# Second score product of 64-wide heads over all 128 rows, with k's low parts copied into both halves of their tile

## The chip, the cores and the metric

The kernel runs on one core of one Trainium2 chip. The metric is the device time of one execution in microseconds; the time of the kernel before is the median of three runs. A profile of one further execution, with a trace of every instruction, was taken by the hardware profiler.

## What is computed

Two transformer blocks on one sequence of 512 tokens and 1024 features, all in float32. The first block joins a sparse attention (compressed, selected and window branches for 16 heads of 64 in four groups of keys and values) with a linear recurrent branch, then a gated feed-forward part. The second block has two layers, each with a feed-forward part, four mixers side by side, and another feed-forward part. Three of the mixers matter here, cut to their score products:

```python
# neighbourhood attention: 4 heads, d = 64, a window of 8 x 32 keys for each column block
logits = jnp.einsum('brcqhd,brkcjhd->brcqhkj', qg, kg,
                    preferred_element_type=jnp.float32) * (d ** -0.5) + bias
# grouped-query attention: 4 heads, 2 of keys and values, d = 64
logits = jnp.einsum('bqngd,bknd->bngqk', qb, k, preferred_element_type=jnp.float32) * scale
# multi-head latent attention: 4 heads, d = 64 + 32 = 96
logits = jnp.einsum('bqhd,bkhd->bhqk', q, k, preferred_element_type=jnp.float32) * scale
```

Each is followed by a softmax and a product with the values. The fourth mixer, differential attention, has heads of 32.

## The kernel before

**Split products.** Every float32 operand of a product is split in two float32r parts, high (ScalarE's copy) and low (VectorE's difference). A product is the sum high x high + high x low + low x high in one PSUM bank. For large weights these are the three matmuls of `feat` (L142 to L144) and `tok_` (L172 to L174), over 128 rows each.

**Scores of 64-wide heads.** The features of a head stand on 64 partitions, so q's two parts share one tile of 128 partitions, [high; low] (`pair_T`, `q_pair`). k's high part stands twice in its tile, [high; high]: ScalarE writes the upper half (L754 in `kdup`, L1515 in `k_both`), POOL copies it to the lower (`again`, L747, called from `kdup`; L1516). k's low part stands only in the upper half of its tile, written by VectorE (L756, L1517); nothing is written in its lower half. The first product, over 128 rows, gives high x high and low x high together. The second takes the upper 64 rows of q's tile and k's low part, high x low, and adds it into the same bank:

- first block: L1571 and L1572, once for each of 16 heads, 2 branches and 4 blocks of queries (128 pairs); the columns are 128, 256, 384 and 512, by block of queries;
- grouped-query attention: L1025 and L1026, 16 pairs of 512 columns in each layer;
- neighbourhood attention: both on L1097, in a loop over k's two tiles with r = 128 and r = 64 rows, 16 pairs of 256 columns in each layer.

Latent attention multiplies over 96 rows (L1224 to L1226), differential attention over 96 rows in one product (L948).

**Order.** In the first block 32 units (group, head, branch) run in turn. In step j of a unit stand the scores and softmax of the next unit for query block j (`soft`), a piece of fill work (`fill.pump`: projections, gates), and the values of this unit (`pv`: four transposes, a split by ScalarE and VectorE, two products). `k_both` of the next group is called in unit 5 of 8, and its tiles are used from unit 7 on. In the second block 16 heads of four mixers run in turn, in the order differential, neighbourhood, grouped-query, latent; a head is prepared in the turn two before its values, its scores run in the turn one before. `kdup` is called at step 2 of that preparation for neighbourhood attention, and at step 0 of every second head for grouped-query attention. Within this order a scheduler sets the place of every instruction on its engine's queue by priorities (`high_priority`) and a simulated timeline. Each engine works its queue in order.

**POOL** in these stretches also splits the low parts of streamed weights (L127, while `attends` is set), scales P by the softmax sums (L777, L1106, L1577) and makes bias tables (L1091, L1562). Tiles for k are taken from a ring of 4 (second block) or 6 (first block) shared by high and low parts.

Of the kernel before, what the change touches and what calls it, by code (L numbers as in the profile page):

```python
# [47 lines left out]
def pick(w, m):  # L48
    """Columns of one 128-wide part, high and low."""
    return w[0][:, m * 128:m * 128 + 128], w[1][:, m * 128:m * 128 + 128]  # L50


def whole(gen):
    """Runs a generator to its end."""
    while True:
        try:
            next(gen)
        except StopIteration as e:
            return e.value


class Fill:
    """Work in small steps that is laid between the steps of other work."""
# [21 lines left out]
class Kern:  # L85
# [8 lines left out]
    # ---------------------------------------------------------------- helpers  # L94
    def weights(self, bufs):
        """A pool for parts of weights in flight."""
        self.wb = bufs
        return self.tc.tile_pool(name="w", bufs=1)
# [4 lines left out]
    def pair(self):  # L103
        """Two banks for a block of products; where no attention runs, its banks take turns with them."""
# [3 lines left out]
    def stream(self, src, K, C):  # L108
        """Loads a block [128, K*C] of weights in parts of four k-tiles, split into two float32r parts."""
# [26 lines left out]
    def feat(self, ps, w, ks, mh, ml, start=True, stop=True):  # L136
        """ps[feature, token] += w(k).T @ m(k), three passes."""
# [8 lines left out]
    def feat2(self, w, ks, mh, ml):  # L146
        """Two banks [feature, token] for a block of 256 features."""
        return whole(self.feat2_(w, ks, mh, ml))
# [10 lines left out]
    def tok(self, w, K, C, xh, xl):  # L159
        """Four [token, feature] parts of two banks: x(tb).T @ w. The first product of a bank marks all of it unwritten,  # L160
        so that the first of its second half overwrites."""
# [20 lines left out]
    def rstd(self, ss, width, n, tag, bufs=2):  # L182
        """(ss / width + eps) ** -0.5 on [128, n]."""
# [7 lines left out]
    def rstd_v(self, ss, width, n, tag, bufs=2):  # L191
        """The same on the vector engine: a first guess from the bits, then three steps of Newton's method."""
# [11 lines left out]
    def tokred(self, acc, rhs, n):  # L204
        """Sums acc [128 features, 512 tokens] over features against rhs [128, n] -> psum [128 tok, 4, n]."""
# [6 lines left out]
    def bcast(self, r, pool=None, tag="rB", bufs=1):  # L212
        """r [128 tok, 4] -> [128, 512] with r along the free axis in each partition."""
# [13 lines left out]
    def norm_k(self, xk, k, g, xh, xl, acc):  # L227
        """One k-tile of a norm: squares into acc, x*g split into xh, xl."""
# [21 lines left out]
    # ---------------------------------------------------------------- program  # L250
# [28 lines left out]
    def skews(self, pa):  # L279
        """Rows in DRAM that a strided read turns into Toeplitz tables: the negated T5 bias of each head over the  # L280
        distance from -511 to 511, 128 times."""
# [16 lines left out]
    def skews_na(self):  # L298
        """The neighbourhood bias 16 times."""
# [64 lines left out]
    def norm(self, gname, g0):  # L364
        """The norm of x by one gain: called for each k-tile once it is final, then finished."""
# [12 lines left out]
    def outproj(self, w_o, mh, ml, norm):  # L378
        """x += w_o.T @ m, and the norm that follows."""
# [10 lines left out]
    def gate(self, br, j, t):  # L390
        """Twice the sigmoid, less one, of a block of a branch's gates into t."""
# [6 lines left out]
    def merge(self, pm, got, ah, al, lh, ll, mh, ml):  # L398
        """The gated sum of both branches; got: the gates that there are."""
# [24 lines left out]
    def lru(self, pl, po, yT):  # L424
# [4 lines left out]
        # softplus(-lambda), with log1p(e) = 2 artanh(e / (2 + e))  # L429
# [88 lines left out]
    def ffn(self, f, half, norm):  # L518
        """x += (half) * swiglu, and the norm that follows."""
# [36 lines left out]
    # ---------------------------------------------------------------- second block  # L556
# [18 lines left out]
    def final_norm(self, l):  # L575
        """x = rmsnorm(x) * final, and the norm by ffn1 that follows it in the next layer."""
# [52 lines left out]
    def mix(self, px, l, norm):  # L629
        """The four mixers: their projections and w_out rows fill the tensor engine between the steps of attention,  # L630
        in which the softmax of one head runs beside the values of the head before."""
# [21 lines left out]
        # ---- projections  # L653
        def proj(src, C, evac):
            """A token-major projection: evac(tb, psum, r) takes each block of 128 tokens."""
# [21 lines left out]
        def sums(t, n, d):  # L677
            """Sums of squares over d of t [128, 4, n, d]."""
# [11 lines left out]
        def rope_n(rope, t, tb, n, d):  # L690
            """Rotates t [128, n, d] of one block of tokens in place."""
# [10 lines left out]
        # ---- attention  # L702
        def transp(src, n=128):
            """Four transposes of src(tb) [128 tok, n] into one bank [n, 512 tok]."""
# [5 lines left out]
        def times(a, n):  # L710
            """a [128, d] n times side by side."""
# [17 lines left out]
        def pair_T(src, hh, of=same, to_=same):  # L729
            """[hi; lo] of one of two heads from a bank with both."""  # L730
# [6 lines left out]
        def kpair(src, g=None, n=128):  # L737
            """[hi] and [lo], times a gain by row."""
# [10 lines left out]
        def kdup(src, b, g=None):  # L749
            """Of 64 rows from a bank, at b: [hi; hi] and [lo]."""  # L750
# [5 lines left out]
            V.scalar_tensor_tensor(kl[0:64], src, g, kh[0:64].bitcast(FT), op0=OP.mult, op1=OP.subtract)  # L756
            return kh, kl
# [8 lines left out]
        def plain(ps, t, qb):  # L766
            """Softmax of the unbiased scores of one block of queries."""
# [26 lines left out]
        def finish(y, hh, of=same, to_=same):  # L794
            """Adds the two halves of O into the rows of one head in y()."""
# [8 lines left out]
        def ypair(n=2):  # L804
            """Lazily made pairs of heads."""
# [21 lines left out]
        def ynorm(y, beta):  # L827
            """rmsnorm over the 256 features of two pairs, split."""
# [3 lines left out]
        def wout(parts):  # L832
            """x += w_out rows of the mixers i, each from Y: two pairs (hi, lo)."""
# [13 lines left out]
        def wout_b(Y, sum_b):  # L847
            """The last mixer's rows, whose norm's factor follows; the first pair's products run ahead."""
# [822 lines left out]
def host(inputs):  # L1671
# [4 lines left out]
    A = {}  # L1676
# [146 lines left out]
```

## Time and profile before

| | us |
|---|---|
| median of three runs | 3197.78 |
| lowest and highest | 3192.75 and 3217.31 |
| span of the profiled execution | 3202.2 |

The page gives no time of the profiled execution other than its span, from the first to the last instruction. The engines' busy times over that span are TensorE 3109.5 us (97%), its weight loads 2569.8 us (80%), VectorE 1797.9 (56%), ScalarE 1396.5 (44%) and POOL 676.2 (21%).

PE is TensorE's matmuls, PEld its weight loads, DVE VectorE, ACT ScalarE, POOL GpSimd, SP SyncE. A matmul's duration runs from its start to a modelled end and holds its latency, so that a busy PE need not be PE at its peak; how close matmuls follow each other is read from their starts. `128*128 128x512` is a stationary tile of 128 rows by 128 columns and a moving one of 128 rows by 512 columns. PEclk is the granted clock of TensorE as a share of full speed. The column behind `|` or in brackets is idle time of the engine before an instruction, and what ended it; "issue" is time in which it waited for nothing that the profile shows.

### The profile page before, as it was taken

How to read it: one execution, taken by the hardware profiler on the slowest of the kernel's cores; microseconds unless marked ns; L12 is line 12 of the kernel's file. 1: busy time of each engine (PE TensorE's matmuls, PEld its weight loads, DVE VectorE, ACT ScalarE, POOL GpSimd, SP SyncE). 2: the span in 40 equal slices, each digit the busy share in tenths (PEclk: the TensorE clock that was granted, in tenths of full speed). 3: DMA queues.
4: the chain of work that ended last, by engine and by line, in shares of the span. 5: the costliest groups of instructions: out<-in, count | busy, mean ns of one | idle time of the engine just before them, and what ended most of it. 6: DMA issues, size and time to landing. Idle time of an engine off the chain costs nothing.

```text
span 3202.2 us, 41597 instructions
## 1 busy us (share of the span) xinstructions
PE 3109.5 (97%) x15289; PEld 2569.8 (80%) x15289; DVE 1797.9 (56%) x3520; ACT 1396.5 (44%) x2753; POOL 676.2 (21%) x726
## 2 busy tenths in 40 slices
PE   7999999999999999999999999999999999899998
PEld 6887777878888888889877788888888987678886
DVE  7566766454443444437886644445443698764433
ACT  4566665233332333336665433333333566543332
POOL 3355641010000000016652100010000556310000
PEclk9999988999999999999899999999999999999999
DMA  4211111342233332333221223322233322123332
GB/s 146 87 57 53 47 46 40 99 140 98 94 98 96 96 99 97 95 111 93 75 55 34 86 99 95 96 92 99 99 96 95 109 81 59 34 73 99 99 96 82
DMA packets 105268, 275.84 MB, mean 86 GB/s; under 512 B 27172, under 2 KB 36900, under 8 KB 104904
## 3 DMA queue, kind: packets, MB, share of 16 engines
q1 hardware_dynamic: 105064, 273.18, 27.0%
q8 instruction: 120, 1.97, 0.3%
q14 instruction: 84, 0.69, 0.1%
HBM read 268.93 MB, written 6.80 MB: 86 GB/s over the span
## 4 chain that ended last, share of the span: by engine, by line
PE 76%; issue 12%; DVE 8%; ACT 2%; POOL 1%; DMA 1%; DVEq 0%; SPq 0%; ACTq 0%; POOLq 0%
PE ps_mm L142 8%; PE ps_mm L144 8%; PE ps_mm L143 8%; PE ps_s L143 6%; PE ps_s L144 6%; PE ps_s L142 6%; PE ps_t L144 6%; PE ps_t L143 6%; PE ps_t L142 6%; PE ps_mm L172 2%; PE ps_mm L174 2%; PE ps_mm L173 2%; PE ps_s L1572 1%; PE ps_t L1590 1%; PE ps_t L787 1%
## 5 line engine op out<-in xcount | busy, mean ns | idle before, releaser
L125 ACT ACTIVATE hi<-raw 128x512 fp32r<-128x512 f32 (+2 forms) x952 | 594.8, 627 | 1356.2 <-PE ps_s L143 407.5
L127 DVE TENSOR_TENSOR lo<-raw,hi 128x512 fp32r<-128x512 f32 x782 | 547.7, 702 | 929.4 <-ACT hi L125 918.6
L142 PE MATMUL ps_mm<-xh,hi 128*128 128x512 f32 (+1 forms) x792 | 311.4, 394 | 2.3 <-ACT hi L125 2.3
L144 PE MATMUL ps_mm<-xh,lo 128*128 128x512 f32 (+1 forms) x792 | 310.1, 393 | 1.5 <-POOL lo L127 1.5
L143 PE MATMUL ps_mm<-xl,hi 128*128 128x512 f32 (+1 forms) x792 | 310.1, 391 | 0.0
L238 POOL TENSOR_TENSOR acc<-acc,sq 128x512 f32<-128x512 f32 x49 | 74.4, 1518 | 1051.3 <-issue 525.6
L142 PE MATMUL ps_s<-xh,hi 128*128 128x512 f32 x656 | 253.2, 391 | 7.5 <-ACT hi L125 7.5
L143 PE MATMUL ps_s<-xl,hi 128*128 128x512 f32 x656 | 257.3, 392 | 3.1 <-DVE xl L243 3.0
L172 PE MATMUL ps_mm<-hi,xh 128*128 128x256 f32 (+1 forms) x896 | 259.2, 292 | 0.9 <-ACT tk L664 0.7
L127 POOL TENSOR_TENSOR lo<-raw,hi 128x512 fp32r<-128x512 f32 (+2 forms) x170 | 226.1, 1334 | 150.9 <-ACT hi L125 142.5
L173 PE MATMUL ps_mm<-lo,xh 128*128 128x256 f32 (+1 forms) x896 | 256.5, 289 | 0.0
L144 PE MATMUL ps_s<-xh,lo 128*128 128x512 f32 x656 | 256.3, 391 | 0.0
L174 PE MATMUL ps_mm<-hi,xl 128*128 128x256 f32 (+1 forms) x896 | 256.1, 290 | 0.1
L142 PE MATMUL ps_t<-xh,hi 128*128 128x512 f32 x608 | 236.8, 390 | 0.0
L143 PE MATMUL ps_t<-xl,hi 128*128 128x512 f32 x608 | 236.6, 389 | 0.0
L144 PE MATMUL ps_t<-xh,lo 128*128 128x512 f32 x608 | 235.9, 390 | 0.7 <-DVE lo L127 0.5
L172 PEld LDWEIGHTS ps_mm<-hi,xh 128*128 128x128 f32 x896 | 173.7, 195 | 5.5 <-ACT tk L664 1.3
L144 PEld LDWEIGHTS ps_mm<-xh,lo 128*128 128x128 f32 (+1 forms) x792 | 148.5, 187 | 34.8 <-POOL lo L127 2.4
L142 PEld LDWEIGHTS ps_mm<-xh,hi 128*128 128x128 f32 (+1 forms) x792 | 148.6, 188 | 34.4 <-ACT hi L125 2.6
L173 PEld LDWEIGHTS ps_mm<-lo,xh 128*128 128x128 f32 x896 | 173.8, 195 | 2.9 <-issue 1.2
L174 PEld LDWEIGHTS ps_mm<-hi,xl 128*128 128x128 f32 x896 | 172.4, 194 | 4.2 <-issue 1.6
L143 PEld LDWEIGHTS ps_mm<-xl,hi 128*128 128x128 f32 (+1 forms) x792 | 148.6, 188 | 31.9 <-issue 1.4
(539 smaller groups left out, 6739.9 us busy)
## 6 DMA issues: line engine op xcount, KB each, us to landing
raw<-in_w_g SPq DMA_DIRECT2D x110, 512.0 KB
raw<-in_w_u SPq DMA_DIRECT2D x110, 512.0 KB
raw<-in_w_d SPq DMA_DIRECT2D x108, 512.0 KB
raw<-in_w_o SPq DMA_DIRECT2D x24, 512.0 KB
raw<-in_w_c SPq DMA_DIRECT2D x16, 512.0 KB
raw<-in_w_m SPq DMA_DIRECT2D x16, 512.0 KB
raw<-in_w_a SPq DMA_DIRECT2D x12, 512.0 KB
raw<-in_w_d SPq DMA_DIRECT2D x20, 256.0 KB
```

Of the source, the lines that this page charges most:

```text
L125: nc.scalar.activation(hi[:, :c], x, AF.Copy)
L127: eng.tensor_tensor(lo[:, :c], x, hi[:, :c].bitcast(FT), op=OP.subtract)
L142: mm(ps, wh, mh(km), start=s, stop=False)
L143: mm(ps, wh, ml(km), start=False, stop=False)
L144: mm(ps, wl, mh(km), start=False, stop=e)
L172: mm(out[tb], h, wh, start=k == 0 and tb % 2 == 0, stop=False)
L173: mm(out[tb], h, wl, start=False, stop=False)
L174: mm(out[tb], o, wh, start=False, stop=k == K - 1 and tb % 2 == 1)
L238: nc.gpsimd.tensor_tensor(acc, acc, sq, op=OP.add)
L787: PE.transpose(ps[:, qb * 128:qb * 128 + 128], P[qb][:, kb * 128:kb * 128 + 128], ident)
L1572: PE.matmul(ps[:, :L], q[0:64], kl[0:64, :L], start=False, stop=True)
L1590: PE.transpose(tps[:, (qb - kb) * 128:(qb - kb + 1) * 128], P[qb][:, kb * 128:kb * 128 + 128], ident)
```

## The change

The tile of k's low part is filled in both halves: after VectorE has written the upper 64 rows, POOL copies them to the lower 64 rows. The second product then runs over 128 rows of q's tile [high; low] and k's tile [low; low] and gives high x low plus low x low. The first products are as they were. The rest of the diff takes out comments and docstrings, with the line numbers kept up to the edit.

```diff
@@ -747,13 +747,14 @@
         def kdup(src, b, g=None):
...
             V.scalar_tensor_tensor(kl[0:64], src, g, kh[0:64].bitcast(FT), op0=OP.mult, op1=OP.subtract)
+            again(kl[64:128], kl[0:64])
             return kh, kl
@@ -1023,14 +1024,14 @@
                     PE.matmul(ps, qT, kh, start=True, stop=False)
-                    PE.matmul(ps, qT[0:64], kl[0:64], start=False, stop=True)
+                    PE.matmul(ps, qT, kl, start=False, stop=True)
@@ -1093,8 +1094,7 @@
                     for n, kk in enumerate(t["k"]):
-                        r = 128 - 64 * n
-                        PE.matmul(ps[:, :256], qT[0:r], kk[0:r].rearrange("p (r c) -> p r c", c=64)[:, :, c0:c0 + 32],
+                        PE.matmul(ps[:, :256], qT, kk.rearrange("p (r c) -> p r c", c=64)[:, :, c0:c0 + 32],
                                   start=n == 0, stop=n == 1)
@@ -1515,10 +1515,11 @@
                 V.scalar_tensor_tensor(kl[0:64], src, gb, kh[0:64].bitcast(FT), op0=OP.mult, op1=OP.subtract)
+                G.tensor_scalar(kl[64:128], kl[0:64].bitcast(FT), 1.0, 1.0, op0=OP.mult, op1=OP.mult)
                 t["kT"].append((kh, kl))
@@ -1569,7 +1570,7 @@
             PE.matmul(ps[:, :L], q, kh[:, :L], start=True, stop=False)
-            PE.matmul(ps[:, :L], q[0:64], kl[0:64, :L], start=False, stop=True)
+            PE.matmul(ps[:, :L], q, kl[:, :L], start=False, stop=True)
```

## Rows read from the trace of the kernel before

**Rows 1.** The page: the chain that ended last, shares of the span by engine

```profile
PE 76%; issue 12%; DVE 8%; ACT 2%; POOL 1%; DMA 1%; DVEq 0%; SPq 0%; ACTq 0%; POOLq 0%
```

**Rows 2.** Stretches: length, busy time and count by engine, granted clock, DMA share, GB/s

```profile
core 0: us, PE busy (x) PEld busy (x) DVE busy (x) ACT busy (x) POOL busy (x), PEclk, DMA share, GB/s
130.00:530.00 400.00, 392.82 (x2037) 303.67 (x2036) 263.42 (x748) 261.53 (x614) 200.23 (x211) 0.96 0.14 47
1550.00:1680.00 130.00, 121.67 (x722) 100.00 (x721) 112.96 (x306) 83.32 (x202) 85.53 (x118) 0.93 0.22 60
```

**Rows 3.** Chain that ended last, by line: 130 to 530 us, then 1550 to 1680

```profile
by line: PE ps_s L1572 11.0%; PE ps_mm L142 9.8%; PE ps_mm L144 9.5%; PE ps_mm L143 9.3%; PE ps_t L1590 9.1%; PE ps_s L1571 6.3%; PE ps_mm L172 5.5%; PE ps_mm L174 5.4%; PE ps_mm L173 5.3%; PE ps_o L1594 3.5%; PE ps_n L1594 3.2%; PE ps_o L1
...
by line: PE ps_mm L172 6.7%; PE ps_mm L174 6.1%; PE ps_mm L173 6.0%; issue 5.2%; PE ps_s L1097 4.4%; DVE st L773 4.3%; DVE PTl L225 4.2%; DVE tk L697 3.1%; PE ps_s L1026 3.0%; PE ps_t L1116 2.9%; PE ps_t L787 2.4%; DVE xT L845 2.3%; PE ps_o
```

**Rows 4.** Timeline (start us, duration us, engine, instruction): a dense stretch, 512 columns

```profile
1400.03 0.39 PE L142 MATMUL ps_t<-fh,hi 128*128 128x512 f32 x1
1400.03 0.19 PEld L143 LDWEIGHTS ps_t<-fl,hi 128*128 128x128 f32 x1
...
1400.93 0.39 PE L143 MATMUL ps_t<-fl,hi 128*128 128x512 f32 x1
```

**Rows 5.** Timeline: two products of latent attention, over 96 rows

```profile
1727.57 0.40 PE L1225 MATMUL ps_s<-kT,qT 96*128 96x512 f32 x1
1727.80 0.40 PE L1226 MATMUL ps_s<-kT,qT 96*128 96x512 f32 x1
```

**Rows 6.** Timeline: full-height steps of 256 columns (first row) and 128

```profile
231.87 0.28 PE L1593 MATMUL ps_o<-PTh,Vt 128*128 128x256 f32 x1
...
1621.55 0.27 PE L1125 MATMUL ps_o<-PTl,Vg 128*128 128x128 f32 x1
1621.66 0.28 PE L1124 MATMUL ps_o<-PTh,Vg 128*128 128x128 f32 x1
```

**Rows 7.** Timeline: pairs of 512, 256 and 128 columns, then one of L1097

```profile
220.97 0.47 PE L1571 MATMUL ps_s<-kT,qT 128*128 128x512 f32 x1
221.38 0.18 PEld L1572 LDWEIGHTS ps_s<-kT,qT 64*128 64x128 f32 x1 [0.24 <-issue]
221.38 0.50 PE L1572 MATMUL ps_s<-kT,qT 64*128 64x512 f32 x1
221.81 0.19 PEld L173 LDWEIGHTS ps_mm<-lo,xh 128*128 128x128 f32 x1 [0.25 <-issue]
221.81 0.39 PE L173 MATMUL ps_mm<-lo,xh 128*128 128x256 f32 x1
...
231.99 0.28 PE L1571 MATMUL ps_s<-kT,qT 128*128 128x256 f32 x1
232.20 0.38 PE L1572 MATMUL ps_s<-kT,qT 64*128 64x256 f32 x1
232.51 0.38 PE L172 MATMUL ps_mm<-hi,xh 128*128 128x256 f32 x1
...
140.48 0.31 PE L1571 MATMUL ps_s<-kT,qT 128*128 128x128 f32 x1
140.72 0.32 PE L1572 MATMUL ps_s<-kT,qT 64*128 64x128 f32 x1
140.97 0.33 PE L1590 MATMUL ps_t<-ident,P 128*128 128x128 f32 x1
...
1564.00 0.68 PE L1097 MATMUL ps_s<-kT,qT 128*128 128x256 f32 x2
1564.61 0.39 PE L172 MATMUL ps_mm<-hi,xh 128*128 128x256 f32 x1
```

**Rows 8.** By line: POOL's copies of k, VectorE's low part; ns min/median/max, first, last

```profile
L1516 POOL TENSOR_SCALAR kT<-kT x8: 612/616/1534, 114.4 to 426.4; 64x512 fp32r<-64x512 f32 x8
...
L747 POOL TENSOR_SCALAR kT<-kT x28: 610/614/1077, 1474.6 to 2686.1; 32x512 fp32r<-32x512 f32 x16, 64x512 fp32r<-64x512 f32 x12
...
L756 DVE SCALAR_TENSOR_TENSOR kT<-ps_t,gn,kT x8: 733/734/736, 1554.1 to 2657.3; 64x512 fp32r<-64x512 f32 x8
```

**Rows 9.** The page: POOL's splits of weights, count, busy us, mean ns

```profile
L127 POOL TENSOR_TENSOR lo<-raw,hi 128x512 fp32r<-128x512 f32 (+2 forms) x170 | 226.1, 1334 | 150.9 <-ACT hi L125 142.5
```

## The prediction

> **What bounds the kernel now.** I read the chain that ended last first: TensorE's matmuls hold 76% of it, VectorE 8%, the rest is small [rows 1]. So work taken off TensorE should shorten the run, but only where the chain stands on TensorE in the stretch concerned. The changed products run in two kinds of stretch: the attention of the first block, 130 to 530 us, and, once in each layer of the second block, neighbourhood and grouped-query attention (1550 to 1680 us in layer 0; layer 1 repeats it). The view by stretches shows the reader who else is busy there: in the first, VectorE 263 and ScalarE 262 of 400 us; in the second, VectorE 113 of 130 us, which is 87% [rows 2]. The chain of these stretches alone, by line, says how much of it is the products to be changed: L1572 11.0% in the first; L1097 4.4% and L1026 3.0% in the second, where VectorE's lines come up between them [rows 3].
>
> **What the second product costs beyond its columns.** In the timeline of the dense stretches a full-height matmul of 512 columns starts every 0.225 us (1400.03 to 1400.93, four steps), and the weights of the next one are loaded while it runs: both rows begin at 1400.03 [rows 4]. Products over 96 rows keep that pace, 0.23 us from L1225 to L1226, although both add into one bank and use the same stationary tile [rows 5]. 256 columns take 0.12 us and 128 columns 0.11 us [rows 6, 7].
>
> The products over 64 rows don't keep it. L1571 starts at 220.97, and the 64-row load of L1572 only at 221.38, as L1571's modelled end (221.44) is reached; the load itself is idle 0.24 us before, released by nothing the profile names. The next full-height load, at 221.81, sits idle 0.25 us in the same way [rows 7]. So the array runs empty twice for each pair: on the way into the 64 rows and on the way out. Shape is what sets these rows apart, since [rows 5] share everything else with them.
>
> **Price of a pair**, first product to the start of what follows, less two full-height steps [rows 4, 6, 7]; each is one of 32 alike:
> - 512 columns: 0.84 - 0.45 = 0.39 us. 256: 0.52 - 0.24 = 0.28. 128: 0.49 - 0.22 = 0.27. For 384 I take the middle of 256 and 512, 0.335. Block one has 32 of each: 1.275 x 32 = 40.8 us.
> - Neighbourhood attention, 256 columns: both products take 0.61 us (1564.00 to 1564.61), less 0.24 is 0.37; 16 pairs in each layer, 11.8 us together.
> - Grouped-query attention, 512 columns, 16 pairs in each layer: at the 0.39 of block one's pair, 12.5 us.
>
> Together 65.1 us of TensorE's time, if the second product over 128 rows steps like any full-height one. The trace of before does not hold this very product; the bounds are 0 returned (it is slow for another reason) and all 65.1. The rows nearest to it are the 96-row products, full-height by their pace, so I take all of it off TensorE's own time.
>
> The Trainium skill's page "TensorE: Matmul & The Clock Gate", Part 3, says that a weight load overlaps a matmul in flight only when their row groups differ. By that rule a full-height load after a full-height product could not run ahead, the edit would bring nothing, and the sum would be 0 instead of 65.1; the trace disagrees, since such a load starts with the matmul before it at 1400.03 [rows 4].
>
> **How much reaches the end.** From the end of the first product to its own end L1572 takes 0.44 us at 512 columns, 0.31 at 256, 0.25 at 128 [rows 7], the middle 0.375 at 384: 1.375 x 32 = 44.0 us. The chain of that stretch gives it 11.0% of 400 us, 44.0 us as well [rows 3]: all 128 are on it. In the second kind of stretch L1026 would be 16 x 0.44 = 7.0 us and L1097, both products, 16 x (0.12 + 0.31) = 6.9 us; the chain has 3.9 and 5.7 us [rows 3], 9.6 of 13.9, or 0.69. When TensorE is faster other waits come up. Between nothing lost and half lost I choose by how full the next engine becomes: in block one 263 us of VectorE in some 360 us is 73%, so I keep 0.85; in block two VectorE is already at 87%, so I keep 0.75. What is late next there is the softmax chain, VectorE's reduction and ScalarE's exponential ahead of the values' products. The sum: 40.8 x 0.85 = 34.7, and 24.3 x 0.69 x 0.75 = 12.6, together 47.3 us.
>
> **What it adds.** Twenty copies of 64 x 512 on POOL: 8 at L1516's place (two for each of four groups), 4 in grouped-query and 8 in neighbourhood attention. Each costs what the copy of the high part does, 0.61 to 0.62 us [rows 8], 12.3 us in all. POOL is busy 200 of 400 us and 86 of 130 us [rows 2], so its time is covered by its own idle time. The new wait is in its queue: the copy can start only when VectorE has made the low part (0.73 us, L756), and behind it stand the split of streamed weights (L127, 1334 ns each, [rows 9]), which TensorE's fill work waits for, and the scaling of P. The second product now waits for POOL instead of VectorE. Worst case, with nothing between: 0.73 + 0.62 = 1.35 us for each of the 20 tiles, 27 us; best case, 0. In block one the program puts the tile two units ahead of its use and I take 0; in block two's 12 tiles it is half a head to a head ahead, and I take 0.2 us each, 2.4 us. No load, DMA or VectorE instruction is added, and tiles come free as before, after the last score product. The matmul count stays.
>
> The sum is 47.3 - 2.4 = 44.9 us off the profiled span of 3202.2, 3157.3; the median of the runs shown, 3197.78, lies 4.4 us under that span, so I put the run at **3153 us**.
>
> **Rivals.**
> - *The chain moves to the softmax.* The drains go, but less than half of the 65.1 us reaches the end: 5 to 32 us gained, 3166 to 3193. For it: VectorE's 87% in block two. Against it: block one has most of the gain, and there L1572 is wholly on the chain.
> - *The load is not the reason*, and a full-height second product stays slow: 3198. For it, only the page's rule above. Against it, [rows 4, 5].
> - *Slower: the low parts come late.* All 20 copies end after TensorE is ready. The 47.3 us are used up at 2.4 us for each tile, and the run is 1% slower (32 us) at 4.0 us for each. That is POOL three splits behind (3 x 1.33) at every tile. One copy did take 1534 ns against a median of 616 [rows 8], so something holds POOL now and then, but 2.4 us each is more than any row shows. At 4 us each: 3230. The page "SBUF — State Buffer" of the Trainium skill ("SBUF: two separate sides") says that VectorE with two SBUF inputs and GpSimd exclude each other for a whole instruction; the 1534 ns fit it, and no run here shows the cause.
> - *More than the sum.* The granted clock is 0.96 and 0.93 of full speed (2.4 GHz) in the mean of the two stretches [rows 2], so for part of them it was at the lower level, 1.2 GHz; if a denser TensorE keeps the upper one, up to 4% of 400 us comes on top of the 44.9: 61 us or more, 3137 and under.
>
> **How the numbers follow.** A measurement of this kernel tells about 1% (32 us) from no change. My forecast, a gain of 32 to 66 us, gets 0.75; the softmax 0.13; no effect 0.03; late low parts 0.05, most of it past 1%; more than the sum 0.04. Faster is 0.75 + 0.04 = 0.79; slower 0.04; the rest, 0.17, is within 1%. The range runs from 3132 (all 65.1 us) up to 3184 (14 us gained, the softmax taking most of it) and leaves out about 0.15.
>
> **What would show it.** In the profile after, L1026, L1572 and L1097 as 128-row products with mean times near those of L1025, L1571 and the other L1097 shape; their loads starting under the product before, with no idle "issue" time ahead; the pair at 512 columns about 0.45 us from first start to the next; block one's attention shorter by some 35 us, each layer of block two by some 5. Waits of TensorE for POOL's copies at L747 would show the added wait; longer waits for VectorE at L225, L773 or L1574 the softmax. The prediction is wrong if the pairs stay at 0.8 us, or if they shorten and the stretches don't.

## The result and the profile after

The changed kernel takes **3164.64 us** (median of 4 runs, 3161.95 to 3165.43) where the kernel before took 3196.93 beside it (4 runs, 3192.75 to 3217.31). The ratio is 0.9881, 95% interval 0.9852 to 0.991: some 38 us less. The medians differ by 32 us and the shortest executions by 31: the four executions of the kernel before spread over 25 us, those of the kernel after over 3.5, so that the size of the gain depends on what is compared. The profiled execution has a span of 3162.1 us, against 3202.2.

First the page of the kernel after: busy time of each engine, then the chain that ended last, by engine.

```profile
PE 3041.4 (96%) x15289; PEld 2554.9 (81%) x15289; DVE 1797.1 (57%) x3520; ACT 1396.7 (44%) x2753; POOL 686.8 (22%) x746
...
PE 80%; DVE 10%; ACT 3%; POOL 2%; issue 2%; DMA 1%; SPq 0%; DVEq 0%; POOLq 0%; ACTq 0%
```

Against [rows 1] "issue", time in which the chain waited for nothing that the profile names, fell from 12% to 2%; the rest moved to TensorE and VectorE (8% to 10%). Next the view by stretches, columns as in [rows 2]: the first block's attention, which now ends 37 us earlier, and neighbourhood with grouped-query attention of layer 0.

```profile
core 0: us, PE busy (x) PEld busy (x) DVE busy (x) ACT busy (x) POOL busy (x), PEclk, DMA share, GB/s
130.00:490.00 360.00, 346.78 (x2051) 293.50 (x2050) 260.01 (x744) 257.71 (x610) 200.91 (x217) 0.98 0.16 52
1510.00:1645.00 135.00, 114.79 (x738) 101.44 (x738) 116.46 (x313) 84.80 (x206) 91.05 (x125) 0.91 0.21 57
```

In the first stretch about as many matmuls as before (2051 against 2037) take 40 us less. In the second 738 take 135 us, where 722 took 130. The chain of the first stretch by line:

```profile
by line: PE ps_t L1591 7.3%; PE ps_mm L142 6.8%; PE ps_mm L144 6.7%; PE ps_mm L143 6.4%; issue 5.4%; PE ps_mm L173 5.0%; PE ps_mm L172 4.9%; PE ps_mm L174 4.9%; PE ps_s L1572 4.9%; PE ps_s L1573 4.1%; PE ps_n L1595 2.9%; PE ps_n L1594 2.3%;
```

The second product stands one line lower than before (L1573 now, L1572 then, and so on for every line behind `kdup`): 4.1% of 360 us, 15 us, where it held 44 us [rows 3]. In the timeline (start us, duration us) two pairs of the first block, matmuls first, then the weight loads of the first pair:

```profile
163.44 0.36 PE L1572 MATMUL ps_s<-kT,qT 128*128 128x256 f32 x1
163.64 0.28 PE L1573 MATMUL ps_s<-kT,qT 128*128 128x256 f32 x1
163.76 0.34 PE L1595 MATMUL ps_o<-PTl,Vt 128*128 128x384 f32 x1
...
165.22 0.50 PE L1572 MATMUL ps_s<-kT,qT 128*128 128x512 f32 x1 [0.66 <-DVE st L1575]
165.56 0.39 PE L1573 MATMUL ps_s<-kT,qT 128*128 128x512 f32 x1
165.79 0.28 PE L1594 MATMUL ps_o<-PTh,Vt 128*128 128x256 f32 x1
...
163.41 0.19 PEld L1572 LDWEIGHTS ps_s<-kT,qT 128*128 128x128 f32 x1
163.52 0.19 PEld L1573 LDWEIGHTS ps_s<-kT,qT 128*128 128x128 f32 x1
163.64 0.19 PEld L1595 LDWEIGHTS ps_o<-PTl,Vt 128*128 128x128 f32 x1
```

L1573's load starts at 163.52, under L1572, which began at 163.44; no load is idle ahead of it. The pair of 256 columns takes 0.32 us to the next start (163.76 - 163.44) where it took 0.52 [rows 7], the one of 512 columns 0.57 where it took 0.84. In the second pair the first product's step is 0.34 us, not 0.23, because it starts after a wait, here 0.66 us for VectorE's L1575.

### The profile page after: what moved, and what is told of

Same layout as the page of the kernel before. It is cut to its first block, busy times and chain, and to the rows that moved or that the text cites. A ratio compares the mean times of both kernels' runs of the same rounds, so it can differ in the third digit from the quotient of the medians.

```text
span 3162.1 us, 41620 instructions
## 1 busy us (share of the span) xinstructions
PE 3041.4 (96%) x15289; PEld 2554.9 (81%) x15289; DVE 1797.1 (57%) x3520; ACT 1396.7 (44%) x2753; POOL 686.8 (22%) x746
## 4 chain that ended last, share of the span: by engine, by line
PE 80%; DVE 10%; ACT 3%; POOL 2%; issue 2%; DMA 1%; SPq 0%; DVEq 0%; POOLq 0%; ACTq 0%
PE ps_mm L142 8%; PE ps_mm L144 8%; PE ps_mm L143 8%; PE ps_s L143 7%; PE ps_s L144 7%; PE ps_s L142 7%; PE ps_t L144 7%; PE ps_t L143 7%; PE ps_t L142 7%; PE ps_mm L172 2%; PE ps_mm L173 2%; PE ps_mm L174 2%; DVE PTl L225 1%; PE ps_t L1591 1%; DVE st L774 1%
```

## The experiments

Each kernel was timed against the kernel before, beside it. e1 to e4, e5 to e8, e9 and e10, and e11 and e12 ran on four different chips, where the kernel before had medians of 3198.34, 3200.93, 3197.68 and 3201.91 us. Within such a group the times compare as they are; across groups the ratios are to be compared. First the list; ratios are to the kernel before, with 95% intervals.

| kernel | edit | median us | ratio |
|---|---|---|---|
| after | the whole change | 3164.64 | 0.9881 (0.9852 to 0.991) |
| e1_block1 | the first block's part alone | 3161.78 | 0.9876 (0.9846 to 0.9906) |
| e2_na | neighbourhood attention's part alone | 3202.35 | 0.9998 (0.9979 to 1.0018) |
| e3_gqa | grouped-query attention's part alone | 3196.33 | 0.9992 (0.997 to 1.0013) |
| e4_copies | the 20 copies alone | 3203.13 | 1.0018 (0.9995 to 1.0041) |
| e5_e_order | after, the bias table's loads kept together | 3153.58 | 0.9854 (0.9835 to 0.9873) |
| e6_rows96 | after, second product over 96 rows | 3164.13 | 0.9884 (0.9862 to 0.9906) |
| e7_twice | before, first block's 64-row product twice | 3221.72 | 1.006 (1.0038 to 1.0082) |
| e8_low_on_act | after, second block's copies on ScalarE | 3152.62 | 0.9854 (0.9834 to 0.9874) |
| e9_order_act | e5 and e8 together | 3159.11 | 0.9849 (0.9804 to 0.9894) |
| e10_order_before | before, with e5's edit | 3199.16 | 0.9995 (0.9972 to 1.0019) |
| e11_no_max | e5, grouped-query softmax without the row maximum | 3146.46 | 0.9829 (0.9806 to 0.9851) |
| e12_no_max_64 | e11, grouped-query second product over 64 rows | 3150.96 | 0.9839 (0.9822 to 0.9856) |

### Which part brings the gain

The change has three parts that stand by themselves: the first block, neighbourhood attention, grouped-query attention. `kdup` is given a flag for its copy, and a product whose low part isn't copied goes back to 64 rows. The edit of e1_block1, against the kernel after; e2_na has the flag off in grouped-query attention, e3_gqa in neighbourhood attention, and both have the first block as before.

```diff
-        def kdup(src, b, g=None):
+        def kdup(src, b, g=None, low=True):
...
-            again(kl[64:128], kl[0:64])
+            if low:
+                again(kl[64:128], kl[0:64])
...
-                    PE.matmul(ps, qT, kl, start=False, stop=True)
+                    PE.matmul(ps, qT[0:64], kl[0:64], start=False, stop=True)
```

> Block one's part of the change alone (its 8 copies and 128 products over 128 rows); neighbourhood and grouped-query attention as in the kernel before. If block one gave all of the gain (its scores are 38 us shorter in the profile after, 40.8 us was the sum of its drains): 36 to 41 us off, ratio 0.987 to 0.989, the same as the whole change. If block two's stretches gave a share as well, less than that: 30 us or under.

> Neighbourhood attention's part alone: its 8 copies on POOL and 32 products over 128 rows. Theory 1, POOL and the queues behind it set that stretch and the copies make it late: 8 to 16 us slower, the stretch from its first to its last score product some 7 us longer in each layer, with TensorE waiting for VectorE at L1097. Theory 2, the softmax chain set it all along and takes what the drains give back: within 3 us of before, no stretch longer. The prediction's sum (drains returned at 0.52): 6 us faster.

> Grouped-query attention's part alone: its 4 copies on POOL and 32 products over 128 rows. The prediction's sum, 12.5 us of drains at 0.52: 6 us faster. If the softmax chain takes it all: within 2 us of before.

The first block alone gives 0.9876, what the whole change gives. Each of the second block's parts gives nothing that its interval tells from 1. Neighbourhood attention, measured from the start of its first score product to that of its last, even grew: 60.7 and 59.1 us in the two layers of before, 67.8 and 66.1 of after, 69.2 and 65.3 of e2_na. That is the stretch that its first theory expected, but the 8 to 16 us of the whole time did not follow.

For e3_gqa the ratio hides something. TensorE's granted clock, in the mean of an execution, was 0.976 or less in six of its ten executions, and in six of the 25 of the kernel before beside it; in its profile the low clock stands in the first block (0.92 from first to last score product), which its edit leaves alone. At 0.979 to 0.981 its median is 3191.1 us (four executions) against 3196.8 (twelve), 5.7 us less, and three of its executions are shorter than the shortest of the 25 (3192.12). For e2_na the same comparison gives 3197.0, no difference. The profiles point the same way. The rows hold the stretch from the first neighbourhood product of layer 0 to the end, in e10_order_before (whose second block has the products of before), e3_gqa and the kernel after:

```profile
1549.90:3194.30 1644.40, 1585.33 (x7789) 1315.66 (x7787) 938.32 (x1771) 694.67 (x1347) 327.52 (x376) 0.98 0.27 83
```

```profile
1574.40:3211.10 1636.70, 1577.97 (x7789) 1317.42 (x7787) 934.91 (x1771) 693.93 (x1347) 327.98 (x380) 0.98 0.26 84
```

```profile
1517.10:3162.10 1645.00, 1567.75 (x7789) 1316.32 (x7787) 939.61 (x1774) 696.80 (x1347) 333.01 (x387) 0.97 0.27 83
```

So grouped-query attention's part by itself is worth some 6 to 8 us at like clock, about its share of the forecast, as far as a choice of executions made afterwards and one profile each can show it. In the change as a whole block one's term arrived and the second block's did not.

### Are the copies to blame

e4_copies, against the kernel before, has the copies, and its products still run over 64 rows:

```diff
+            again(kl[64:128], kl[0:64])
...
+                G.tensor_scalar(kl[64:128], kl[0:64].bitcast(FT), 1.0, 1.0, op0=OP.mult, op1=OP.mult)
```

> The 20 copies on POOL alone: all score products as in the kernel before, the second one over 64 rows. It prices the copies without any drain returned. Theory 1 (POOL's queue sets neighbourhood attention): 10 to 20 us slower, nearly all of it in the two neighbourhood stretches, block one within 2 us. Theory 2 (the copies lie in POOL's idle time): within 3 us of before everywhere.

The run measured 1.0018 (0.9995 to 1.0041), and the neighbourhood stretches stay at 60.8 and 60.0 us. The 20 copies cost somewhere between nothing and 13 us (3.7 us by the executions at a granted clock of 0.979 to 0.981) and don't make that stretch longer. In the kernel after TensorE waits for a copy by itself, at L747, 1.7 us at most (two waits of the load, 1.2 us, and two of the product, 0.5).

### What made neighbourhood attention longer

The waits of the kernel after, 1510 to 1592 us (who waits, for what: us in total, times, longest), lead there in two steps:

```profile
PEld ps_s L1097 <- DVE st L1102: 5.8, 3, 4.6
...
DVE P L1102 <- POOL nab L1092: 4.6, 1, 4.6
POOL nab L1092 <- issue: 4.2, 1, 4.2
```

TensorE waits for a bank that VectorE's L1102 must empty; VectorE waits for the bias table `nab` from POOL; and POOL waits for nothing that the profile names. In layer 1 (2575 to 2645 us) the profile does name it:

```profile
POOL nab L1092 <- DMA E<-rpd: 3.3, 1, 3.3
```

`nab` reads E, a tile that SyncE fills with eight loads for each head. The timeline of SyncE's queue and of POOL in the kernel after, layer 0:

```profile
1561.53 3.15 SPq L1076 DMA_DIRECT2D E<-rpd  x7
...
1576.59 0.51 SPq L1076 DMA_DIRECT2D E<-rpd  x1
...
1582.23 2.09 POOL L1092 TENSOR_TENSOR nab<-namask,E 128x256 f32<-128x256 f32 x3 [4.18 <-issue]
```

Seven of E's loads go in at 1561.53, the eighth only at 1576.59, behind eight loads of values, two of rope rows and two of weights; POOL's table follows 5.64 us later. In layer 1 three go in at 2621.75 and the other five from 2631.69 on, behind eleven others. In the kernel before the same eight stood together, as this row of its SyncE timeline shows:

```profile
1600.62 4.19 SPq L1075 DMA_DIRECT2D E<-rpd  x8
```

The kernel e2_na, where neighbourhood attention alone is changed, shows the same split:

```profile
1600.37 3.15 SPq L1077 DMA_DIRECT2D E<-rpd  x7
...
1617.06 0.47 SPq L1077 DMA_DIRECT2D E<-rpd  x1
```

No line of the program asks for that order; the scheduler set it, from its simulated timeline of the changed kernel. The test gives E's loads the priority that the program uses elsewhere for urgent work (e5_e_order, against the kernel after; e10_order_before has the same edit against the kernel before):

```diff
-                            nc.sync.dma_start(E[rr * 16:rr * 16 + 16],
+                            with hot():
+                                nc.sync.dma_start(E[rr * 16:rr * 16 + 16],
```

> The whole change, with a higher scheduling priority for the eight loads of a neighbourhood head's bias table (E), so that they stand together in SyncE's queue as in the kernel before. In the profile after, the last of the fourth head's loads is issued some 15 us after the first, behind values' loads and a weight load, and the scores of that head wait. Theory 1, that order is why neighbourhood attention became 7 us longer in each layer: its stretch from first to last score product comes back to 58 to 61 us in both layers (before 60.7 and 59.1; after 67.8 and 66.1). Theory 2, the copies in POOL's queue are why: it stays at 65 to 69 us. For the whole time: 3150 if the lost 14 us all reach the end, within 4 us of the changed kernel (3160 to 3168) if VectorE's softmax sets block two.

The result is 3153.58 us, 0.9854. The loads stand together, and the products of L1097 (one line lower here) run at a median of 286 ns, 350 in the kernel after. The rows are from the timeline of SyncE in e5_e_order, and from its view of that line (duration min/median/max in ns, first and last start):

```profile
1559.88 3.63 SPq L1077 DMA_DIRECT2D E<-rpd  x8
```

```profile
L1098 PE MATMUL ps_s<-kT,qT x32: 280/286/580, 1515.5 to 1571.5; 128*128 128x256 f32 x32
```

Neighbourhood attention now takes 56.1 and 56.3 us, less than the 60.7 and 59.1 of before and than the 58 to 61 expected. The price of the split order is best read on one chip: e6_rows96 (below), where the loads are still split, took 3164.13 us (3162.22 to 3166.74), 10.6 us more than e5_e_order (3152.03 to 3157.77). The traces agree throughout: in the three kernels with one head's loads split (after, e2_na, e6_rows96) neighbourhood attention takes 65.3 to 69.2 us, in all eleven others 55.6 to 61.5. The same edit on the kernel before shows whether the priority is a gain of its own:

> The kernel before with the higher priority for the bias table's loads alone. There those loads stand together already. Theory: the change broke an order that was sound, so the same edit is worth 0 to 3 us here (3194 to 3200). If the priority helps whatever the change does: 8 to 11 us, 3187 to 3192.

It measured 0.9995 (0.9972 to 1.0019): nothing. So the order was not a fault of the kernel before; the change brought it.

A second way round moves the second block's copies from POOL to ScalarE, (e8_low_on_act, against the kernel after), and a third does both (e9_order_act, this and e5's edit):

```diff
-            again(kl[64:128], kl[0:64])
+            S.activation(kl[64:128], kl[0:64].bitcast(FT), AF.Copy)
```

> The whole change with block two's twelve low copies made by ScalarE instead of POOL (block one's stay on POOL). Theory: POOL's queue makes neighbourhood attention late, so its stretch comes back to 58 to 62 us, and the run gains 0 to 10 us on the changed kernel: 3153 to 3165. Rival: the softmax on VectorE and ScalarE sets these stretches and ScalarE's extra 12 x 0.6 us lengthens them: 3165 to 3175.

> Both repairs together: the bias table's loads kept in one piece, and block two's low copies on ScalarE. Each alone ran at 3153. If both mend the same lateness of neighbourhood attention: again 3150 to 3155. If the copies cost POOL's queue something of their own: 3143 to 3149.

e8_low_on_act measured 3152.62 us, the same as e5. That does not speak for POOL as the cause: in the order that the scheduler made of this kernel E's eight loads stand together too. The row is from SyncE's timeline in e8_low_on_act:

```profile
1560.15 3.97 SPq L1076 DMA_DIRECT2D E<-rpd  x8
```

e9_order_act, 0.9849 (0.9804 to 0.9894), adds nothing to either by its ratio, as it should if both mend one fault; its median of 3159.11, on another chip, lies above the 3150 to 3155 expected.

### Is it the height of the product, or the change to it

e6_rows96, against the kernel after, makes the second products over 96 rows, and its copies are of 32 rows. In the first block:

```diff
-            PE.matmul(ps[:, :L], q, kl[:, :L], start=False, stop=True)
+            PE.matmul(ps[:, :L], q[0:96], kl[0:96, :L], start=False, stop=True)
```

> The whole change with the second product over 96 rows instead of 128, and copies of 32 rows instead of 64 (the product high x low is whole; of low x low a half is added). If the drain comes from the change to the half-height array, 96 rows are as good as 128: within 3 us of the changed kernel, 3162 to 3167, and 0.23 us steps at 512 columns. If it comes from the rows that differ between neighbouring products, the drains are back: near 3197, 0.8 us for a pair.

The 96-row products give the time of the 128-row ones, 3164.13 against 3164.64 (ratios 0.9884 and 0.9881), so 96 rows do as well as 128, although the height still changes from one product to the next, and half as many rows copied make no difference. E's loads are split here as in the kernel after (seven and one in layer 0).

e7_twice, against the kernel before, makes the first block's 64-row product twice, so that its scores hold high x low twice:

```diff
             PE.matmul(ps[:, :L], q[0:64], kl[0:64, :L], start=False, stop=False)
+            PE.matmul(ps[:, :L], q[0:64], kl[0:64, :L], start=False, stop=True)
```

> The kernel before with block one's second score product made twice in a row, both over 64 rows (the scores so hold high x low twice). It measures whether each 64-row product costs a drain or only the change of height. Change of height: one more step of 0.225, 0.173, 0.12 and 0.11 us for each of 32 pairs, 20 us slower. Each 64-row product waits for the one before it to leave: 0.43, 0.37, 0.31 and 0.25 us, 43 us slower.

The ratio of 1.006 is 19 us more, with an interval of 12 to 26: near the 20 us of the added columns, far from the 43 us of a price on each 64-row product. By itself the time would not decide, since the granted clock of 130 to 530 us was 0.94 in this profile and 0.96 in [rows 2]. The timeline of e7_twice shows why, matmuls and then loads:

```profile
285.46 0.40 PE L1571 MATMUL ps_s<-kT,qT 128*128 128x512 f32 x1
285.79 0.50 PE L1572 MATMUL ps_s<-kT,qT 64*128 64x512 f32 x1
286.13 0.39 PE L1573 MATMUL ps_s<-kT,qT 64*128 64x512 f32 x1
286.45 0.50 PE L143 MATMUL ps_mm<-xl,hi 128*128 128x512 f32 x1
...
285.79 0.18 PEld L1572 LDWEIGHTS ps_s<-kT,qT 64*128 64x128 f32 x1 [0.36 <-issue]
285.90 0.19 PEld L1573 LDWEIGHTS ps_s<-kT,qT 64*128 64x128 f32 x1
286.45 0.19 PEld L143 LDWEIGHTS ps_mm<-xl,hi 128*128 128x128 f32 x1 [0.36 <-issue]
```

The second 64-row load starts at 285.90, under the first 64-row product (285.79). Only the first load of 64 rows and the next load of 128 are idle before they start. Over the whole first block it is the same: the view by line has the product of L1572 idle for no named reason 88 times, that of L1573 six times.

```profile
L1572 PE MATMUL ps_s<-kT,qT x128: 322/438/793, 134.7 to 527.4; 64*128 64x128 f32 x32, 64*128 64x256 f32 x32, 64*128 64x384 f32 x32, 64*128 64x512 f32 x32
...
  issue: 22.3, 88
...
L1573 PE MATMUL ps_s<-kT,qT x128: 268/335/626, 134.8 to 528.0; 64*128 64x128 f32 x32, 64*128 64x256 f32 x32, 64*128 64x384 f32 x32, 64*128 64x512 f32 x32
...
  issue: 1.4, 6
```

So the array runs empty between a product of 128 rows and one of 64, once on the way in and once on the way out; between 64 and 64 rows, or 128 and 96, it does not. The Trainium skill has a rule for this in "TensorEngine Tiling (Array Packing)", section Key Properties: a change of tiling mode drains TensorE. This trace agrees if 64 rows are another mode, with 0.36 us of idle load at each change here.

### Where the rest of the second block's gain goes

With the order mended the stretch from the first neighbourhood product to the end takes 1636.1 us in e5_e_order, 8.3 us less than in e10_order_before, where 12.6 less 2.4 was forecast:

```profile
1515.50:3151.60 1636.10, 1568.80 (x7789) 1313.42 (x7787) 942.99 (x1774) 694.35 (x1347) 331.93 (x387) 0.98 0.27 84
```

What is missing, some 2 us, is less than these runs can tell from nothing. But the gain does not stand where it was expected: grouped-query attention, first to last score product, takes 46.3 and 46.4 us in e5_e_order where it took 44.9 and 42.7 before. In the view of e5_e_order by line, its first score product (L1026, layer 0) was idle for this:

```profile
L1026 PE MATMUL ps_s<-kT,qT x16: 389/478/792, 1574.0 to 1620.3; 128*128 128x512 f32 x16
...
  ACT P L776: 9.6, 9
```

9.6 us in nine waits for ScalarE's exponential to free a bank; before there was none. ScalarE in turn stands behind the row maximum on VectorE. If the softmax takes the gain, a softmax with less work must give it back. Two kernels leave the maximum out of grouped-query attention, one with the product over 128 rows and one over 64. First e11_no_max, against e5_e_order:

```diff
-            V.tensor_reduce(mn, ps, axis=AX, op=OP.max, negate=True)
-            S.activation(p, ps, AF.Exp, bias=mn, scale=1.0, accum_out=sm)
+            S.activation(p, ps, AF.Exp, scale=0.1, accum_out=sm)
```

e12_no_max_64, against e11_no_max, which also leaves out grouped-query attention's copies:

```diff
-                    PE.matmul(ps, qT, kl, start=False, stop=True)
+                    PE.matmul(ps, qT[0:64], kl[0:64], start=False, stop=True)
```

> The whole change with the bias table's loads in one piece (3153.6 us) and with less work for VectorE in grouped-query attention: its softmax leaves out the row maximum (16 reductions of 0.68 us in each layer, 21.8 us in all; the exponent is scaled by 0.1 instead, so the output differs). If VectorE sets that stretch (46.3 us in each layer): 8 to 20 us faster, 3134 to 3146. If TensorE or the order of the program sets it: within 3 us of 3153.6.

> As e11_no_max (no row maximum in grouped-query attention), but its second score product over 64 rows again, without its four copies. The difference to e11_no_max is what that mixer's drains, 12.5 us by the prediction's sum, are worth once VectorE is relieved. If VectorE had taken them: this is 6 to 13 us slower than e11_no_max. If they were lost to something else: within 3 us of it.

The stretches of layer 0 from the first grouped-query score product to the last, columns as in [rows 2], one fence for each kernel: before, e5_e_order, e11_no_max, e12_no_max_64.

```profile
1620.30:1665.20 44.90, 41.24 (x211) 29.57 (x209) 40.75 (x105) 35.48 (x85) 23.51 (x33) 1.00 0.12 37
```

```profile
1574.10:1620.40 46.30, 39.20 (x200) 30.60 (x201) 44.41 (x112) 35.72 (x86) 25.86 (x39) 0.93 0.12 38
```

```profile
1574.10:1615.50 41.40, 36.80 (x204) 29.35 (x205) 36.30 (x102) 35.11 (x87) 25.83 (x40) 1.00 0.14 43
```

```profile
1576.20:1620.80 44.60, 42.88 (x202) 31.33 (x200) 35.56 (x101) 36.12 (x90) 25.50 (x40) 0.92 0.13 41
```

e11_no_max measured 0.9829 and 3146.46 us against 0.9854 and 3153.58 for e5_e_order, 7 to 8 us less on different chips: at the edge of the 8 to 20 expected if VectorE set that stretch, and with overlapping intervals. VectorE is busy 44.41 of 46.30 us (96%) in e5_e_order, against 91% before, and TensorE 85% against 92%. Without the maximum VectorE falls to 88% and the stretch to 41.4 us; with 64 rows on top of that it is TensorE that is full again, 42.88 of 44.60 us (96%). The direction is the one the softmax theory wants, but the times don't settle it: the medians, 3146.46 and 3150.96, differ by 4.5 us, under the 6 to 13 of one theory and over the 3 of the other, and the two intervals overlap. And the granted clock differs between these stretches (0.93, 1.00 and 0.92), so part of the difference in length is not VectorE's.

## Why the prediction was right, and where it was wrong

The forecast was 3153 us, and its range of 3132 to 3184 holds the measured 3164.64. The sign, the mechanism and block one's term are right; block two's term did not arrive in the change as it stands, for a reason that none of the rivals named.

**The drains.** Right. The second products are as quick as the first ones: L1573 332 ns against L1572's 339, L1027 393 ns, L1097 286 ns in e5_e_order. No idle "issue" time stands before their loads. The page's rule that the prediction set against this, from "TensorE: Matmul & The Clock Gate", Part 3 of the Trainium skill, would have left the pairs as they were; the load at 163.52 under the product begun at 163.44 contradicts it. One argument for it was misread: L1225 and L1226 [rows 5] do not use the same stationary tile, one takes q's high part and the other its low part. So those rows could not rule out that a second load of the same tile has to wait. L1224 and L1225, which do share one, settle it: 0.23 us there too (1727.34 to 1727.57). So do the pairs of after, whose two products load the same 128 rows of q.

**The price of a pair.** Nearly right in sum, too high at 512 columns. Over every pair of the first block, first start to the next start, the medians by 128, 256, 384 and 512 columns were 0.490, 0.554, 0.722 and 0.834 us before and are 0.276, 0.242, 0.355 and 0.546 after; the differences times 32 give 37.8 us where the forecast had 40.8. At 512 columns the difference is 0.29, like the 0.31 at 256 columns, and not 0.39. The pair from which 0.39 was read starts right behind transposes: the first row stands ahead of it in the kernel before, the others are a pair behind the same L1511 in the kernel after.

```profile
220.73 0.49 PE L1511 MATMUL ps_t<-ident,tk 128*128 128x128 f32 x3
```

```profile
213.14 0.60 PE L1511 MATMUL ps_t<-ident,tk 128*128 128x128 f32 x4
213.50 0.48 PE L1572 MATMUL ps_s<-kT,qT 128*128 128x512 f32 x1
213.81 0.39 PE L1573 MATMUL ps_s<-kT,qT 128*128 128x512 f32 x1
214.05 0.28 PE L173 MATMUL ps_mm<-lo,xh 128*128 128x256 f32 x1
```

Like against like, 0.84 became 0.55. The 0.1 us above the forecast's 0.45 is mostly the slow start behind the transposes, 0.31 us to the second product instead of 0.23; it was there before and stays. Of the 32 such pairs of after, nine start so, seven after a wait as at 165.22, and 15 take 0.23 us to the second product. The same 0.39 was put on grouped-query attention's pairs, so block two's 24.3 us were some 3 us too high as well.

**Block one's share.** Right in size. From the first to the last score product it took 371.4 us before and 333.0 after, 38.4 us less, where 34.7 was forecast. But one stretch of the kernel before's profile ran at half the clock. The rows are the stretch by itself and 21 us of it, in the kernel before; then the same first-to-last stretch in e10_order_before, whose first block is that of before, and in the kernel after:

```profile
133.40:504.80 371.40, 367.44 (x1901) 283.52 (x1899) 247.55 (x714) 248.33 (x586) 196.37 (x207) 0.95 0.14 48
472.00:493.00 21.00, 21.00 (x59) 13.85 (x59) 9.98 (x37) 9.05 (x28) 5.51 (x9) 0.50 0.00 0
```

```profile
134.10:500.30 366.20, 360.24 (x1902) 277.78 (x1900) 248.39 (x715) 248.85 (x586) 196.16 (x207) 0.98 0.15 48
```

```profile
135.20:468.20 333.00, 320.87 (x1900) 271.91 (x1899) 246.37 (x714) 246.01 (x585) 196.27 (x212) 0.98 0.17 53
```

At the same granted clock, 0.98, the difference is 33.2 us, which is 0.81 of 40.8; with the 21 us at half the clock it is 0.94. The 0.85 of the forecast lies between. The rest of the shortfall is seen as waits for VectorE, as the prediction named them: the first products waited for VectorE's L1575 for 9.9 us in 21 waits, as at 165.22, where before it was 3.6 us in nine, and VectorE is now 72% busy in the stretch of 360 us (260.01).

**Block two's share.** This is the step that failed. It put 12.6 us on neighbourhood and grouped-query attention, 10.2 with the copies' cost; from the first neighbourhood product to the end the kernel after takes 1645.0 us, and e10_order_before 1644.4. The prediction priced what the changed instructions cost and named POOL's queue as the one that the copies enter, and it said that no load is added. That is so; but it did not ask what the scheduler would do with the loads that were there. Its new order split the loads of one bias table in each layer (in layer 0 the last behind twelve others in SyncE's queue, in layer 1 the last five behind eleven). Neighbourhood attention became 7 us longer in each layer, and the split cost 10.6 us of the whole time, as far as e6_rows96 against e5_e_order shows it. Mended, e5_e_order takes 8.3 us less than e10_order_before in that stretch, and gains 0.0022 of the kernel's time, 7 us, more than e1_block1; the intervals of these two ratios overlap. So with the order right the forecast's 10.2 us are nearly there, within the noise. That the softmax chain, which the prediction named as what is late next, takes the rest is not shown: its signs are 9.6 us of waits for L776 and VectorE at 96%, but e11 against e12, which should have proved it, did not separate the two.

**POOL's copies.** The term of 2.4 us can't be told from nothing: e4_copies has 0.0018 of the time, 6 us, with an interval from -2 to 13. The rival "the low parts come late" did not come about: 1.7 us of waits at L747 at most.

**The other rivals.** The softmax may have taken part of the gain in the second block, as far as the waits show it. "More than the sum" did not come about in the total, but its premise has some support: in the first block's stretch the granted clock was 0.92 to 0.98 (below 0.96 in five) in the six profiles with 64-row products there, and 0.98 or 0.99 in the eight without. That is worth 5 us between the profiles of before and e10_order_before (371.4 against 366.2), and it fits the 38 us of the ratio against 33 us at like clock. No run shows that the height of the products causes it.

**What stays open.** Why the scheduler's order changed: only the orders themselves were seen. With 64-row products and the copies (e4_copies) the stretch did not grow; with the products at 96 or 128 rows and the copies on POOL E's loads are split; with the copies on ScalarE they are not. Open too is why e3_gqa, with grouped-query attention alone, takes hardly longer from the first neighbourhood product to the end than e5_e_order with both (1636.7 and 1636.1 us).

The quickest kernels that compute all of the reference are e5_e_order and e8_low_on_act, 0.9854 of the time before: by the ratios some 9 us better than the change as it stands, with overlapping intervals, and some 11 us better than e6_rows96 on the same chip.

## What to carry to other kernels

Where two matmuls of one bank differ in the rows they use, compare the start of the second one's weight load with the start of the first product: if the load waits with nothing named, the change of height costs more than the columns, and it can pay, as here, to fill the rows with a copy that does no harm. Where a scheduler orders the queues, a change of a few instructions is also a new order of all others: compare each queue's order with the one before, the DMA queues first, before a missing gain is put down to the engines. And cost the parts of a change that touch different stretches by kernels that carry one part each; here a gain and a loss in one total looked like a gain that was merely short. Before such a part is called worthless, compare executions at like granted clock. And read the price of a pair from more than one place: what stands ahead of it can be in the price.

## What the runs showed of the hardware that was not expected

- The cost goes with the change between 64 rows and the full height, not with the height: a 64-row product right behind a 64-row one has its load covered (285.90 under 285.79). A change between 128 and 96 rows costs nothing that the runs show (ratios 0.9884 with 96 rows, 0.9881 with 128).
- A 512-column product that starts right behind a transpose takes 0.31 us to the next start (213.50 to 213.81; 0.31 to 0.33 in nine pairs of the kernel after), against 0.23 in a dense row.
- In the profile of the kernel before the granted clock was 0.50, the level of 1.2 GHz, for 21 us on end (472 to 493 us), while TensorE was busy all of that time and had been busy in all of the 22 us ahead of it, the clock 0.96 there. The same stretch of e2_na shows it too, and e10_order_before has nothing of the kind there. Before such a stretch is read as the kernel's own, its clock is to be looked at.
